# Modulation in four turns of two feature tiles, with w_cond as the moving operand of float32 products

## The chip, the cores and the metric

The kernel runs on one core of one Trainium2 chip. The core has TensorE (PE in the profile, with its weight loads as PEld), VectorE (DVE), ScalarE (ACT), GpSimd (POOL) and SyncE (SP, which here only issues DMAs), each with a queue of its own that it works off in order, and 16 DMA engines. The metric is the device time of one execution in microseconds, as the median of several runs.

## The reference, cut to what matters

One layer of a decoder step: 1024 prompt rows and 8 sample rows go through a modulation, a wide input projection, and two branches (stick-breaking attention and a state-space layer), which are merged and normalised. The change touches the modulation alone:

```python
def _modulate(x, c, w_cond, b_cond):
    mod = c @ w_cond + b_cond
    shift, scale, gate = jnp.split(mod, 3, axis=-1)
    h = x * (1.0 + scale[:, None]) + shift[:, None]
    return h, gate[:, None]

def _project_in(h, w_in):
    z = h @ w_in
    q, k, v, g_att, u, g_ssm, m_att, m_ssm = jnp.split(z, IN_SPLITS, axis=-1)
```

All is float32; `c` has 9 rows here (one for the prompt, eight for the samples), `w_cond` is 1024 x 3072, of which shift and scale take the first 2048 columns, and `w_in` is 1024 x 8192.

## The kernel before

Activations lie transposed: eight feature tiles `xt` of 128 features x 1032 tokens. After the modulation each is split into two reduced-precision parts, `hi` (a cast on ACT) and `lo` (source minus `hi`, on DVE), by `split_act` (L233), and the projection works with three products: hi x hi, hi x lo, lo x hi. A **job** (`gemm`, L125) makes 128 output features: 72 products with 344 moving columns, nine for each feature tile, into three PSUM tiles `pj`. `Weights` (L93) loads a job's weight slab `w32` (one buffer), casts it to `whi` on ACT and subtracts `wlo` on DVE (two buffers each). `Stream` (L148) hands products of the jobs out: `begin(n)` opens the first n jobs, `head(n)` issues products of them out of turn, `drain` and `weave` do the rest, between the steps of the later stages. The first four jobs are q, k, v and gate of the first head pair.

The modulation (`modulate`, L242) runs in two halves. A half takes eight slabs of `w_cond`, each 256 rows by 512 columns, splits each into `wchi` (ACT) and `wclo` (DVE), and multiplies them with a fixed 128-column stationary `csplit`, which holds `c` in its hi part (columns 0 to 8) and its lo part (columns 32 to 40): 32 products of 512 moving columns for a half. The result, rows `mod`, is copied out by ACT (`modr`, L270), turned into features by small products with the selection `sel` that also add hi and lo rows (`pm`, L277), and applied: `md` (L281, L282) is bias plus value, `xt` is scaled and shifted (L285 on ACT for odd tiles, L287 on DVE for even ones, the sample columns at L288 and L289), and `split_act` makes the two parts. In the second half five products of the first job stand behind each slab (`FILL`), and ten more ahead of `features`; they use the first four feature tiles, `job[1] < KT * 9 // 2`.

PE's order is the order in which the program is written. The other engines' orders are made by the scheduler from readiness and priority, and `high_priority(HURRY)` puts a row ahead. Beside the modulation `ssm_tables` (`tabs`, L350 on) makes tables for the state-space layer out of small DVE steps, POOL products over 1056 columns, and two sines on ACT (L428, L429); its three parts are advanced by `next(tabs)`.

Behind the modulation the first job's result is copied out by ACT (`z`, L581), cast to `qs` (L586), its rest subtracted on POOL (L587); the second job gives `kh` (L611) and, on POOL, `kl` (L613), whose upper or lower half a DMA moves to the other partitions (L614). The first score product of the attention, `z` at L661, needs `kl`.

Of the kernel before, what the change touches and what calls it, by code (L numbers as in the profile page):

```python
# [26 lines left out]
LN_EPS = 1e-5  # L27
MAGIC = 12582912.0
MM = 146.0
W32 = 1  # L30
LAG = 2
EDGE = 2
ORDER = {3: (3, 0, 1, 2), 0: (0,), 2: (0, 2, 1), 1: (1, 0)}
HURRY = 400
WCB = 8
ONACT = (1, 3, 5, 7)
FILL = 5
WQ = "pps"
QUEUES = "sasssasss"
PACE = 155  # L40
# [2 lines left out]
GS = "v"  # L43
LATE = 5.0
AHEAD = 2
FILL2 = 10
DRAIN = 1.6
EARLY = 2
TWO_PI = 6.283185307179586
MULT = [float(j) for j in range(9)] + [8.0 * j for j in range(16)] + [128.0 * j for j in range(8)]  # L50
NM = len(MULT)
# [33 lines left out]
def blk(i, w=128):  # L85
    return slice(w * i, w * i + w)
# [6 lines left out]
class Weights:  # L93


    def __init__(self, nc, pool, bufs, ahead):
        self.nc, self.pool, self.bufs, self.ahead = nc, pool, bufs, ahead
        self.todo, self.ready, self.eng, self.q = deque(), deque(), nc.vector, nc.sync

    def plan(self, slabs):  # L100
        self.todo.extend(slabs)

    def emit(self):
        nc = self.nc
        w32 = self.pool.tile([128, KT * 128], F32, tag="w32", bufs=W32, name="w32")
        self.q.dma_start(w32, self.todo.popleft())
        whi = self.pool.tile([128, KT * 128], F32R, tag="whi", bufs=self.bufs, name="whi")
        wlo = self.pool.tile([128, KT * 128], F32R, tag="wlo", bufs=self.bufs, name="wlo")
        nc.scalar.copy(whi, w32)  # L109
        self.eng.tensor_tensor(wlo, w32, whi.bitcast(F32), ALU.subtract)  # L110
        self.ready.append((whi, wlo))
# [36 lines left out]
class Stream:  # L148
# [24 lines left out]
    def head(self, n):  # L173

        for job in self.begun:
            while n and job[1] < KT * 9 // 2:
                next(job[0])
                job[1] += 1
                n -= 1
                self.left -= MM  # L180
                self.clock += MM

# [59 lines left out]
def modulate(k, sp, ps, io, tabs):  # L242


    nc, S = k.nc, k.stream
    PE, ACT, DVE, SP = nc.tensor, nc.scalar, nc.vector, nc.sync
    ct = sp.tile([128, KT, 9], F32, name="ct", bufs=1)
    SP.dma_start(ct, io["ct"])
    cc = split_c(k, sp, ct)
    todo = deque((q, 1024 * s + 512 * half) for half in range(2) for s in range(2) for q in range(4))  # L250
    ahead, xs = deque(), {}

    def load():
        if todo:
            q, c0 = todo.popleft()
            ahead.append(cond_load(k, sp, io, q, c0, WCB))

    def load_x(half):
        for t in range(4 * half, 4 * half + 4):
            xs[t] = sp.tile([128, NT], F32, tag="xt", bufs=5, name="xt")  # L260
            SP.dma_start(xs[t], io["xt"][t])

    def rows(fill):
        ps_ = ps.tile([128, 512], F32, tag="mod", name="mod")
        for q in range(4):
            cond_product(k, ps_, cc, q, cond_split(k, sp, ahead.popleft(), 2))
            load()
            fill()
        r = sp.tile([64, 512], F32, tag="modr", bufs=2, name="modr")
        ACT.copy(r, ps_[0:64])  # L270
        return r

    def features(half, rs):
        pm = ps.tile([128, 512], F32, tag="mod", name="pm")[:, 0:128].rearrange("p (i s n) -> p i s n", i=4, s=2)
        for i in range(4):
            for s in range(2):
                PE.matmul(pm[:, i, s, 0:9], rs[s][:, blk(i)], sel, start=True, stop=True)  # L277
        for i in range(4):
            t = 4 * half + i
            md = sp.tile([128, 2, 9], F32, tag="md", bufs=2, name="md")  # L280
            DVE.tensor_scalar(md[:, 0], pm[:, i, 0, 0:9], bc[:, t:t + 1], None, op0=ALU.add)  # L281
            DVE.tensor_scalar(md[:, 1], pm[:, i, 1, 0:9], bc[:, 8 + t:9 + t], 1.0, op0=ALU.add, op1=ALU.add)  # L282
            x = xs.pop(t)
            if t in ONACT:
                ACT.activation(x[:, 0:NP], x[:, 0:NP], AF.Identity, scale=md[:, 1, 0:1], bias=md[:, 0, 0:1])  # L285
            else:
                DVE.tensor_scalar(x[:, 0:NP], x[:, 0:NP], md[:, 1, 0:1], md[:, 0, 0:1], op0=ALU.mult, op1=ALU.add)  # L287
            DVE.tensor_tensor(x[:, NP:NT], x[:, NP:NT], md[:, 1, 1:9], ALU.mult)  # L288
            DVE.tensor_tensor(x[:, NP:NT], x[:, NP:NT], md[:, 0, 1:9], ALU.add)  # L289
            k.act_h.append(split_act(k, k.hp, x))  # L290

    for n in range(WCB):
        if n == EARLY:
            next(tabs)
        load()
    sel = sp.tile([64, 9], F32, name="sel", bufs=1)
    SP.dma_start(sel, io["sel"])
    bc = sp.tile([128, 16], F32, name="bc", bufs=1)
    SP.dma_start(bc, io["bc"])
    next(tabs)  # L300
    load_x(0)
    k.w.ahead = 2
    k.w.ensure()
    SP.dma_start(k.ident, io["ident"])
    SP.dma_start(k.hb, io["sb_bias"].broadcast_to((128, H)))
    r = [rows(lambda: None) for _ in range(2)]
    features(0, r)
    load_x(1)
    k.w.ahead = 0
    S.begin(2)  # L310
    r = [rows(lambda: S.head(FILL)) for _ in range(2)]
    S.head(FILL2)
    features(1, r)
    S.head(72)
    k.w.ahead = 1


def split_c(k, sp, ct, tag="csplit"):

    nc = k.nc  # L320
    cc = sp.tile([128, KT, 128], F32R, name="csplit", tag=tag, bufs=1)
# [12 lines left out]
def cond_split(k, sp, w, bufs):
    hi = sp.tile([128, 2, 512], F32R, tag="wchi", bufs=bufs, name="wchi")
    lo = sp.tile([128, 2, 512], F32R, tag="wclo", bufs=bufs, name="wclo")
    k.nc.scalar.copy(hi, w)
    k.nc.vector.tensor_tensor(lo, w, hi.bitcast(F32), ALU.subtract)
    return hi, lo


def cond_product(k, ps_, cc, q, parts):

    for t in range(2):
        for x in parts:
            k.nc.tensor.matmul(ps_, cc[:, 2 * q + t], x[:, t], start=(q == 0 and t == 0 and x is parts[0]),
                               stop=(q == 3 and t == 1 and x is parts[1]))
# [1372 lines left out]
```

## Time and profile before

| what | value |
|---|---|
| median of 3 runs | 1664.44 us (1662.58 to 1669.14) |
| the profiled execution's own time | 1668.55 us |
| span of its trace, first to last instruction | 1666.5 us |
| mean granted TensorE clock | 0.958 |
| ACT busy | 754.0 us (45%) |
| DVE busy | 1265.3 us (76%) |
| POOL busy | 895.0 us (54%) |

A row of a timeline gives the start and the duration in us, the engine, the source line, the operation, output and inputs, the count, and in brackets how long the engine had been idle and on whom it waited. A row of a group gives the count behind an x, the busy time in us with the mean in ns, and the idle time ahead of it. In a table by stages, each engine has its busy us and number of instructions, and the last three columns are the granted clock, the busy share of the DMA engines, and GB/s.

### The profile page before, as it was taken

What the parts mean: (1) busy time and instruction counts of PE and PEld (TensorE: products, weight loads), DVE (VectorE), ACT (ScalarE), POOL (GpSimd) and SP (SyncE); (2) the same over time, 40 slices, a digit from 0 to 9 for tenths busy, and PEclk for the clock granted to TensorE, in tenths of its full rate; (3) what the DMA queues carried; (4) which work ended last, traced back from release to release, by engine and by line L of the source; (5) the groups of instructions that cost most, each with busy time, mean ns of one, the idle gap of its engine ahead of it and who ended that gap; (6) DMA issues with size and microseconds to landing.
All of it is one profiled execution on the core that took longest, in us unless ns stands there. A gap on an engine that the chain in (4) does not pass through costs nothing.

```text
span 1666.5 us, 26016 instructions
## 1 busy us (share of the span) xinstructions
PE 1497.7 (90%) x9257; PEld 1423.4 (85%) x9257; DVE 1265.3 (76%) x2342; ACT 754.0 (45%) x1380; POOL 895.0 (54%) x744
## 2 busy tenths in 40 slices
PE   4899899999999999999989898987988869999997
PEld 3799898989898989899978888887878869999885
DVE  8748888888888888872688878978559994544566
ACT  4466666666676666663333333333352222321200
POOL 3437676767676767664456555456336542122154
PEclk8899999999999999999999999889989989999998
DMA  9233333333333333326689888768355576754322
GB/s 333 71 100 82 81 81 81 81 81 81 82 81 82 81 81 81 81 88 205 214 274 292 261 256 266 256 200 233 113 181 172 188 266 240 250 182 150 105 89 89
DMA packets 164125, 258.72 MB, mean 155 GB/s; under 512 B 45049, under 2 KB 106233, under 8 KB 163867
## 3 DMA queue, kind: packets, MB, share of 16 engines
q1 hardware_dynamic: 137945, 163.62, 32.5%
q0 software_dynamic: 23456, 84.95, 15.9%
q10 hardware_dynamic: 2594, 8.49, 1.9%
q8 instruction: 73, 1.20, 0.3%
q14 instruction: 57, 0.47, 0.1%
HBM read 188.38 MB, written 57.86 MB: 148 GB/s over the span
## 4 chain that ended last, share of the span: by engine, by line
PE 41%; DVE 25%; issue 8%; DMA 5%; ACT 4%; POOL 2%; SPq 0%; DVEq 0%; ACTq 0%; POOLq 0%
PE pj L142 26%; PE f L1403 6%; DVE l_t L895 4%; DVE s_sc L837 3%; DVE ke L672 3%; PE o L707 3%; PE tp L690 2%; DMA s_t<-in_cache_k,s_idx 2%; PE z L661 2%; DVE vs L643 2%; DVE be L673 2%; DVE s_t L832 1%; DMA w<-in_w_in 1%; DVE m L1255 1%; DVE ox L716 1%
## 5 line engine op out<-in xcount | busy, mean ns | idle before, releaser
L142 PE MATMUL pj<-ahi,whi 128*128 128x344 f32 x2112 | 700.9, 333 | 56.9 <-ACT u L981 20.4
L142 PE MATMUL pj<-alo,whi 128*128 128x344 f32 x2112 | 691.3, 329 | 10.3 <-DVE alo L1231 5.8
L142 PE MATMUL pj<-ahi,wlo 128*128 128x344 f32 x2112 | 585.0, 329 | 14.2 <-POOL wlo L110 14.2
L142 PEld LDWEIGHTS pj<-ahi,whi 128*128 128x128 f32 x2112 | 410.3, 194 | 65.6 <-ACT u L981 21.4
L142 PEld LDWEIGHTS pj<-alo,whi 128*128 128x128 f32 x2112 | 410.5, 194 | 15.3 <-DVE alo L1231 6.9
L142 PEld LDWEIGHTS pj<-ahi,wlo 128*128 128x128 f32 x2112 | 385.0, 193 | 17.6 <-POOL wlo L110 15.8
L672 DVE TENSOR_TENSOR_SCAN ke<-ke,eye 128x896 f32<-128x896 f32 (+7 forms) x128 | 214.2, 1674 | 81.9 <-ACT ke L662 81.5
L110 POOL TENSOR_TENSOR wlo<-w,whi 128x1024 fp32r<-128x1024 f32 x53 | 134.2, 2532 | 242.7 <-ACT whi L109 242.4
L109 ACT CAST whi<-w 128x1024 fp32r<-128x1024 f32 x90 | 94.9, 1055 | 162.0 <-PE pj L142 111.3
L662 ACT ACTIVATE ke<-z,nhb 128x448 f32<-128x448 f32 (+2 forms) x192 | 112.0, 583 | 82.6 <-PE z L661 79.2
L673 DVE TENSOR_TENSOR be<-be,ke 128x896 f32<-128x896 f32 (+7 forms) x128 | 128.3, 1003 | 11.7 <-DVE ke L672 0.5
L837 DVE SCALAR_TENSOR_TENSOR s_sc<-s_t,s_q,s_sc 128x512 f32<-128x512 f32 x126 | 112.4, 892 | 22.0 <-issue 9.9
L663 ACT ACTIVATE be<-z,hb 128x448 f32<-128x448 f32 (+2 forms) x192 | 110.7, 577 | 0.0
L816 POOL DMA_INDIRECT s_t<-in_cache_k,s_idx x64 | 71.3, 1114 | 39.8 <-issue 12.8
L690 PE MATMUL tp<-ident,be 128*128 128x128 f32 x576 | 89.4, 273 | 0.0
L495 POOL TENSOR_TENSOR pr<-tab 128x256 f32<-128x256 f32 x32 | 31.1, 972 | 102.4 <-DMA tab<-d_tab 98.8
L693 ACT CAST wthi<-tp 128x512 fp32r<-128x512 f32 x96 | 56.6, 590 | 54.7 <-PE tp L690 52.6
L895 DVE SCALAR_TENSOR_TENSOR l_t<-l_t,l_sc 128x128 f32<-128x128 f32 x256 | 78.5, 366 | 2.3 <-DMA l_t<-in_cache_v,l_idx 2.3
L496 POOL TENSOR_TENSOR pt<-tab 128x256 f32<-128x256 f32 x64 | 77.8, 1216 | 3.1
L574 POOL TENSOR_TENSOR sg<-sg,zg 128x1024 f32<-128x1024 f32 x8 | 22.0, 2746 | 99.2 <-ACT sgs L573 99.2
L1525 ACT ACTIVATE gate<-pj 128x344 f32<-128x344 f32 x72 | 33.0, 459 | 92.2 <-PE pj L142 90.1
L661 PE MATMUL z<-kl,qs 128*128 128x448 f32 (+2 forms) x192 | 66.7, 348 | 3.0 <-DMA kl<-kl 3.0
(320 smaller groups left out, 2865.6 us busy)
## 6 DMA issues: line engine op xcount, KB each, us to landing
w<-in_w_in SPq DMA_DIRECT2D x38, 512.0 KB
w<-in_w_in POOLq DMA_DIRECT2D x26, 512.0 KB
wc<-in_w_cond SPq DMA_DIRECT2D x24, 512.0 KB
gst<-d_gg SPq DMA_DIRECT2D x8, 576.0 KB
x<-in_xr SPq DMA_DIRECT2D x9, 512.0 KB
xt<-in_xt SPq DMA_DIRECT2D x8, 516.0 KB
d_ma<-gate SPq DMA_DIRECT2D x8, 516.0 KB
d_mm<-gate SPq DMA_DIRECT2D x8, 516.0 KB
```

The costliest lines, as they stand in the source:

```text
L109: nc.scalar.copy(whi, w32)
L110: self.eng.tensor_tensor(wlo, w32, whi.bitcast(F32), ALU.subtract)
L142: PE.matmul(ps[c], w[:, blk(t)], x[:, cs(c)], start=(t == 0 and i == 0), stop=(t == KT - 1 and i == 2))
L661: nc.tensor.matmul(z[:, 0:wide], st["q", h][:, blk(i)], x[:, s:s + wide], start=j == 0, stop=j == 1)
L662: nc.scalar.activation(ke[:, s:s + cw], z[:, 0:cw], AF.Sigmoid, bias=k.nhb[:, hd:hd + 1], scale=-0.125)
L663: nc.scalar.activation(be[:, s:s + cw], z[:, 0:cw], AF.Sigmoid, bias=k.hb[:, hd:hd + 1], scale=0.125)
L672: nc.vector.tensor_tensor_scan(rev, rev, self.eye[:, NP - n:][:, ::-1], 0.0, ALU.mult, ALU.add)
L673: nc.vector.tensor_tensor(be, be, ke[:, 1:n + 1], ALU.mult)
L690: PE.transpose(tp[:, 2 * order[a] + e], w[e][:, blk(2 * j + a)], k.ident)
L837: DVE.scalar_tensor_tensor(sc, t, q[:, d - d0:d - d0 + 1], sc, op0=ALU.mult, op1=ALU.add)
L895: nc.vector.scalar_tensor_tensor(t[:, d], t[:, d], 1.0, self.sc, op0=ALU.mult, op1=ALU.mult, accum_out=self.acc[:, j, 8 * c + d:8 * c + d ...
L1403: PE.matmul(pp[c], a[:, token(i)], w[:, blk(c, 512)], start=(t == 0 and a is ah and w is wh), stop=(t == KT - 1 and a is al))
```

## The change

The modulation goes in four turns of two feature tiles. For each turn `load` brings four slabs of `w_cond`, 512 rows by 256 columns, and the two `xt` tiles; twelve slabs and six tiles fit at once. The slabs are not split: they are the moving operand of float32 products whose stationary is the nine columns of `ct`, 16 products of 256 columns for a turn (`product`). The rows are copied out with priority, turned by four small products, and one DVE row with priority makes all values of the turn (`turn`); the scale and shift of the prompt columns is on ACT for all eight tiles. In turns 1 to 3, 18 products of the first two jobs stand between `product` and the small products and 18 behind them, nine a job. The second weight slab is loaded into a tile of the setup pool, so that both slabs are loaded and split early. The three parts of `tabs` start later in the written order.

```diff
     def emit(self):
         nc = self.nc
-        w32 = self.pool.tile([128, KT * 128], F32, tag="w32", bufs=W32, name="w32")
+        self.stage.append(self.stage.pop(0))
+        w32 = self.stage[0].tile([128, KT * 128], F32, tag="w32", bufs=1, name="w32")
...
         for job in self.begun:
-            while n and job[1] < KT * 9 // 2:
+            while job[1] < n:
                 next(job[0])
                 job[1] += 1
-                n -= 1
...
-    cc = split_c(k, sp, ct)
...
+    def load(g):
+        for s in range(2):
+            for half in range(2):
+                w = ws[s, half, g] = sp.tile([128, 4, 256], F32, tag="wc", bufs=WCB, name="wc")
+                c0 = 1024 * s + 256 * g
+                SP.dma_start(w, io["w_cond"][512 * half:512 * half + 512, c0:c0 + 256].rearrange("(t p) f -> p t f",
+                                                                                                 p=128))
+        for t in (2 * g, 2 * g + 1):
+            xs[t] = sp.tile([128, NT], F32, tag="xt", bufs=XTB, name="xt")
             SP.dma_start(xs[t], io["xt"][t])
...
+    def product(g):
         ps_ = ps.tile([128, 512], F32, tag="mod", name="mod")
-        for q in range(4):
-            cond_product(k, ps_, cc, q, cond_split(k, sp, ahead.popleft(), 2))
-            load()
-            fill()
...
+        for s in range(2):
+            for t in range(KT):
+                PE.matmul(ps_[0:9, blk(s, 256)], ct[:, t], ws[s, t // 4, g][:, t % 4], start=t == 0, stop=t == KT - 1)
+        rows[g] = sp.tile([9, 512], F32, tag="modr", bufs=2, name="modr")
+        with k.tc.high_priority(HURRY):
+            ACT.copy(rows[g], ps_[0:9])
+
+    def turn(g):
+        pm = ps.tile([128, 512], F32, tag="mod", name="pm")[:, 0:36].rearrange("p (i s n) -> p i s n", i=2, s=2)
+        for s in range(2):
+            for i in range(2):
+                PE.matmul(pm[:, i, s], rows[g][:, blk(2 * s + i)], sel, start=True, stop=True)
+        md = sp.tile([128, 2, 2, 9], F32, tag="md", bufs=2, name="md")
+        with k.tc.high_priority(HURRY):
+            DVE.tensor_tensor(md, pm, bcs[:, 2 * g:2 * g + 2].unsqueeze(3).broadcast_to([128, 2, 2, 9]), ALU.add)
+        for i in range(2):
+            x = xs.pop(2 * g + i)
+            ACT.activation(x[:, 0:NP], x[:, 0:NP], AF.Identity, scale=md[:, i, 1, 0:1], bias=md[:, i, 0, 0:1])
+            DVE.tensor_tensor(x[:, NP:NT], x[:, NP:NT], md[:, i, 1, 1:9], ALU.mult)
+            DVE.tensor_tensor(x[:, NP:NT], x[:, NP:NT], md[:, i, 0, 1:9], ALU.add)
             k.act_h.append(split_act(k, k.hp, x))
...
+    load(0)
...
+    k.w.ahead = 2
+    k.w.stage.append(sp)
+    k.w.ensure()
+    k.w.stage.remove(sp)
+    load(1)
     next(tabs)
+    load(2)
...
+    product(0)
+    turn(0)
+    load(3)
     k.w.ahead = 0
     S.begin(2)
-    r = [rows(lambda: S.head(FILL)) for _ in range(2)]
-    S.head(FILL2)
-    features(1, r)
-    S.head(72)
+    for g in range(1, 4):
+        product(g)
+        S.head(18 * g - 9)
+        turn(g)
+        S.head(18 * g)
+        if g == 1:
+            next(tabs)
     k.w.ahead = 1
```

Three places show the new orders. The first is PE's beginning. Before, this is where the first half ends and the second begins: the last split product of the first half, the eight small products, the first slab of the second half, and the first products of a job (`pj`).

```order
L346 MATMUL mod<-wclo,csplit 128x512
L277 MATMUL pm<-sel,modr 128x9 x8
L346 MATMUL mod<-wchi,csplit 128x512
L346 MATMUL mod<-wclo,csplit 128x512
L346 MATMUL mod<-wchi,csplit 128x512
L346 MATMUL mod<-wclo,csplit 128x512
L142 MATMUL pj<-ahi,whi 128x344
L142 MATMUL pj<-alo,whi 128x344
L142 MATMUL pj<-ahi,wlo 128x344
```

In the changed kernel these are PE's first rows (L263 is `product`, L272 the small products, L140 a job's product):

```order
L263 MATMUL mod<-wc,ct 9x256 x16
L272 MATMUL pm<-sel,modr 128x9 x4
L263 MATMUL mod<-wc,ct 9x256 x16
L140 MATMUL pj<-ahi,whi 128x344
L140 MATMUL pj<-alo,whi 128x344
L140 MATMUL pj<-ahi,wlo 128x344
```

Ahead of the first product of a job there stood 32 split products for the first half and four for the second, and now 32 float32 products.

The second place is ACT at the end of the first two jobs; `pj_408` to `pj_410` are the first job's results before, `pj_506` and `pj_507` the second's, and `qs` is what POOL waits for.

```order
L581 COPY z32_686<-pj_408 128x344
L581 COPY z32_686<-pj_409 128x344
L581 COPY z32_686<-pj_410 128x344
L586 CAST qs_690<-z32_686 64x1024
L586 CAST qs_693<-z32_686 64x1024
L602 COPY zs_696<-z32_686 128x8
L581 COPY z32_740<-pj_506 128x344
L581 COPY z32_740<-pj_507 128x344
```

In the changed kernel `pj_247` to `pj_249` are the first job's, `pj_259` to `pj_261` the second's:

```order
L578 COPY z32_625<-pj_247 128x344
L578 COPY z32_625<-pj_248 128x344
L578 COPY z32_625<-pj_249 128x344
L578 COPY z32_661<-pj_259 128x344
L578 COPY z32_661<-pj_260 128x344
L578 COPY z32_661<-pj_261 128x344
L583 CAST qs_629<-z32_625 64x1024
L583 CAST qs_632<-z32_625 64x1024
```

The casts to `qs` have moved from ahead of the second job's copies to behind them.

The third place is DVE ahead of the last values of the modulation. Before, `md_534` is the first of the second half, and the rows ahead of it (`sm`, L453 to L461) are small steps of the tables.

```order
L338 TENSOR_TENSOR wclo_498<-wc_338,wchi_497 128x1024
L453 TENSOR_SCALAR sm23_602<-tab_117 128x32
L454 TENSOR_TENSOR sm24_603<-sm23_602,sm1_118 128x32
L456 TENSOR_TENSOR sm24_603<-sm24_603,sm25_604 128x32
L457 TENSOR_TENSOR sm26_605<-sm24_603,sm22_601 128x32
L459 TENSOR_TENSOR sm25_604<-sm23_602,sm2_119 128x32
L458 TENSOR_TENSOR sm24_603<-tab_117,sm1_118 128x32
L460 TENSOR_TENSOR sm24_603<-sm24_603,sm25_604 128x32
L461 TENSOR_TENSOR sm27_606<-sm24_603,sm22_601 128x32
L281 TENSOR_SCALAR md_534<-pm_525,bc_141 128x9
```

In the changed kernel `md_519` holds the values of the last turn; `tg_371` and `tt_372` are 1056-column steps of the tables, and `tab_152` (L434) is a product that POOL makes behind the first sine.

```order
L234 TENSOR_TENSOR alo_456<-xt_172,ahi_455 128x1032
L422 TENSOR_SCALAR tg_371<-tf_370 128x1056
L376 TENSOR_SCALAR tt_372<-tg_371 128x1056
L434 TENSOR_SCALAR tab_152<-tab_152 128x32x9
L452 TENSOR_TENSOR sm25_561<-tab_152,sm2_154 128x32
L275 TENSOR_TENSOR md_519<-pm_514,bcs_123 128x36
L279 TENSOR_TENSOR xt_224<-xt_224,md_519 128x8
L279 TENSOR_TENSOR xt_226<-xt_226,md_519 128x8
```

The slabs' splits are gone from DVE, and two rows of the tables that wait for POOL now stand directly ahead of the last values.

More of the change, by code (lines that the diff above doesn't have):

```diff
@@ L29 @@
 MM = 146.0
-W32 = 1
 LAG = 2
@@ L34 @@
 HURRY = 400
-WCB = 8
-ONACT = (1, 3, 5, 7)
-FILL = 5
+WCB = 12
+XTB = 6
 WQ = "pps"
@@ L45 @@
 AHEAD = 2
-FILL2 = 10
 DRAIN = 1.6
-EARLY = 2
 TWO_PI = 6.283185307179586
@@ L98, in __init__ @@
         self.todo, self.ready, self.eng, self.q = deque(), deque(), nc.vector, nc.sync
+        self.stage = [pool]
     def plan(self, slabs):
@@ L248, in modulate @@
     SP.dma_start(ct, io["ct"])
-    cc = split_c(k, sp, ct)
[L250 to L260, printed above, removed]
+    ws, xs, rows = {}, {}, {}
@@ L261, in load_x @@
             SP.dma_start(xs[t], io["xt"][t])
-    def rows(fill):
+    def product(g):
         ps_ = ps.tile([128, 512], F32, tag="mod", name="mod")
-        for q in range(4):
-            cond_product(k, ps_, cc, q, cond_split(k, sp, ahead.popleft(), 2))
-            load()
-            fill()
[L269 to L289, printed above, removed]
-            k.act_h.append(split_act(k, k.hp, x))
@@ L292, in modulate @@
[L292 to L297, printed above, removed]
+        for s in range(2):
[4 more added lines that the diff above has]
+            ACT.copy(rows[g], ps_[0:9])
@@ L298, in modulate @@
+    load(0)
     bc = sp.tile([128, 16], F32, name="bc", bufs=1)
     SP.dma_start(bc, io["bc"])
+    bcs = sp.tile([128, KT, 2], F32, name="bcs", bufs=1)
+    DVE.tensor_copy(bcs[:, :, 0], bc[:, 0:KT])
+    DVE.tensor_scalar(bcs[:, :, 1], bc[:, KT:], 1.0, None, op0=ALU.add)
+    sel = sp.tile([9, 9], F32, name="sel", bufs=1)
+    SP.dma_start(sel, io["sel"][0:9])
+    k.w.ahead = 2
[3 more added lines that the diff above has]
+    load(1)
     next(tabs)
-    load_x(0)
@@ L302, in modulate @@
-    k.w.ahead = 2
-    k.w.ensure()
+    load(2)
     SP.dma_start(k.ident, io["ident"])
     SP.dma_start(k.hb, io["sb_bias"].broadcast_to((128, H)))
-    r = [rows(lambda: None) for _ in range(2)]
-    features(0, r)
-    load_x(1)
+    product(0)
+    turn(0)
+    load(3)
     k.w.ahead = 0
     S.begin(2)
-    r = [rows(lambda: S.head(FILL)) for _ in range(2)]
-    S.head(FILL2)
-    features(1, r)
-    S.head(72)
+    for g in range(1, 4):
[5 more added lines that the diff above has]
+            next(tabs)
```

## The prediction

> **What bounds the kernel now.** I read the page's busy line and the shares of its chain of waits first.
>
> ```profile
> PE 1497.7 (90%) x9257; PEld 1423.4 (85%) x9257; DVE 1265.3 (76%) x2342; ACT 754.0 (45%) x1380; POOL 895.0 (54%) x744
> PE 41%; DVE 25%; issue 8%; DMA 5%; ACT 4%; POOL 2%; SPq 0%; DVEq 0%; ACTq 0%; POOLq 0%
> ```
>
> PE is busy nine tenths of the span, so most of the kernel can't be moved by a change of the modulation. Next I cut the front into windows at the ends of its stages (first split products, second slabs, first `features`, second half, end of the first job, first score product; two of the seven rows are left out).
>
> ```profile
> 0.00:16.00 16.00, 8.41 (x17) 5.22 (x17) 9.56 (x27) 7.01 (x7) 0.20 (x4) 1.00 0.81 268
> ...
> 24.40:38.70 14.30, 0.79 (x1) 0.29 (x1) 14.23 (x34) 9.07 (x9) 9.43 (x4) 0.57 1.04 382
> 38.70:62.40 23.70, 17.91 (x68) 15.21 (x69) 19.52 (x16) 10.96 (x11) 14.12 (x8) 0.76 0.23 78
> 62.40:80.50 18.10, 16.49 (x96) 15.69 (x96) 13.65 (x35) 8.07 (x9) 8.72 (x9) 0.91 0.26 101
> ...
> 97.10:140.00 42.90, 42.86 (x272) 42.35 (x273) 28.35 (x30) 30.73 (x62) 17.37 (x18) 0.96 0.18 55
> ```
>
> PE (the second number) is idle in the front: 7.6 us of the first 16, 13.5 of 24.4 to 38.7, where DVE is busy 14.23 of 14.30. From 97.1 on it is full: 42.86 of 42.90. So the hinge is the end of the front, and I ask the timeline what ends it.
>
> ```profile
> 82.81 4.86 POOL L587 TENSOR_TENSOR qs<-z,qs 64x1024 fp32r<-64x1024 f32 x2 [10.53 <-issue]
> 87.89 5.58 POOL L613 TENSOR_TENSOR kl<-z,kh 64x1024 fp32r<-64x1024 f32 x2 [0.21 <-ACT kh L611]
> 97.14 0.44 PE L661 MATMUL z<-kl,qs 128*128 128x448 f32 x1 [3.04 <-DMA kl<-kl]
> ```
>
> POOL idles 10.53 us, takes `qs` at 82.81, then `kl`; a DMA moves `kl`, and PE waits 3.04 us for it until 97.14. From POOL's `qs` to that product it is 14.3 us, and this stretch stays as it is. All orders behind it are the old ones. So I date the new POOL `qs` and shift the end by the difference, one for one.
>
> **The change part by part.** Removed on DVE and ACT are the splits and casts of 16 slabs.
>
> ```profile
> L338 DVE TENSOR_TENSOR wclo<-wc,wchi 128x1024 fp32r<-128x1024 f32 x16 | 21.6, 1358 | 5.1 <-ACT wchi L337 5.0
> L346 PE MATMUL mod<-wclo,csplit 128*128 128x512 f32 x32 | 17.6, 550 | 12.8 <-DVE wclo L338 12.6
> L346 PE MATMUL mod<-wchi,csplit 128*128 128x512 f32 x32 | 16.8, 526 | 15.4 <-ACT wchi L337 15.4
> L337 ACT CAST wchi<-wc 128x1024 fp32r<-128x1024 f32 x16 | 16.7, 1044 | 17.5 <-PE mod L346 11.3 <-DMA wc<-in_w_cond 6.3
> ```
>
> DVE loses 21.6 us, ACT 16.7, and PE 64 split products (34.4 us of busy time). Their waits, 12.8 and 15.4 us behind DVE and ACT, go with them. PE gains 64 float32 products of 256 columns. None stands in this trace; the nearest rows have 512 columns, and two records each, so that one float32 product appears as two.
>
> ```profile
> 8.56 0.63 PE L346 MATMUL mod<-wclo,csplit 128*128 128x512 f32 x1
> 8.99 0.63 PE L346 MATMUL mod<-wchi,csplit 128*128 128x512 f32 x1
> 20.22 0.40 PE L346 MATMUL mod<-wclo,csplit 128*128 128x512 f32 x1
> 20.46 0.39 PE L346 MATMUL mod<-wchi,csplit 128*128 128x512 f32 x1
> 1197.45 1.02 PE L1160 MATMUL ycr<-gst,ssr 128*128 128x512 f32 x2
> 1198.31 1.02 PE L1160 MATMUL ycr<-tt,ni 128*128 128x512 f32 x2
> 1200.21 1.02 PE L1168 MATMUL ypk<-ec,pick 128*8 128x512 f32 x2 [0.88 <-DVE ec L1163]
> ```
>
> From start to start a split product takes 0.43 us early and 0.24 later: the clock is at half speed in the beginning. A float32 product of 512 columns takes 0.86 (1197.45 to 1198.31), also 1.02 with a stationary of eight columns, so 256 columns should take half of 0.86: **0.43 at full clock, 0.86 at half**. A turn of 16 is 6.9 or 13.8 us; all 64 are 27.5 or 55.
>
> Next the slabs, since products now wait for DMA alone.
>
> ```profile
> 5.18 1.04 ACT L337 CAST wchi<-wc 128x1024 fp32r<-128x1024 f32 x1 [3.08 <-DMA wc<-in_w_cond]
> DMA packets 828, 1.60 MB, mean 399 GB/s; under 512 B 48, under 2 KB 48, under 8 KB 828
> DMA packets 753, 1.05 MB, mean 263 GB/s; under 512 B 48, under 2 KB 560, under 8 KB 753
> ```
>
> The first slab is there at 5.18. The DMA rows are the windows 10:14 and 91:95. A slab of 0.52 MB in 2 KB runs takes 0.52 MB / 399 GB/s = 1.3 us. The new slabs have runs of 1 KB; the nearest window, with 560 of 753 packets below 2 KB, moved 263 GB/s, so 2.0 us is the upper bound. I take 1.5, nearer to the first, because the second window was not asked for more than it moved. The last slab of turn 1 lands behind seven new slabs, two weight slabs and two `xt` tiles, the latter four also 0.5 MB each: 5.2 + 7 x 1.5 + 4 x 1.33 = 21.0 (19.6 to 24.5 with the bounds).
>
> Now the walk. Rows for its steps:
>
> ```profile
> L270 ACT COPY modr<-mod 64x512 f32<-64x512 f32 x4 | 2.3, 580 | 4.0 <-PE mod L346 4.0
> 64.66 1.95 PE L277 MATMUL pm<-sel,modr 64*128 64x9 f32 x16
> L285 ACT ACTIVATE xt<-xt,md 128x1024 f32<-128x1024 f32 x4 | 5.0, 1240 | 9.8 <-DVE md L282 9.8
> L236 ACT CAST ahi<-xt 128x1032 fp32r<-128x1032 f32 x8 | 8.1, 1051 | 1.8 <-DVE xt L289 1.8
> L581 ACT COPY z<-pj 128x344 f32<-128x344 f32 x6 | 2.5, 447 | 0.1
> L237 DVE TENSOR_TENSOR alo<-xt,ahi 128x1032 fp32r<-128x1032 f32 x8 | 9.5, 1221 | 0.0
> 79.47 0.32 PE L142 MATMUL pj<-ahi,whi 128*128 128x344 f32 x1
> 79.63 0.32 PE L142 MATMUL pj<-alo,whi 128*128 128x344 f32 x1
> 98.63 0.49 PE L142 MATMUL pj<-alo,whi 128*128 128x344 f32 x1
> 98.92 0.49 PE L142 MATMUL pj<-ahi,wlo 128*128 128x344 f32 x1
> ```
>
> 1. Turn 0: 8 products at half clock and 8 at full are 10.3 us, from 5.2 to **15.5** (14.0 to 19 if the clock rises sooner, or not at all). The copy 0.58 and the small products 1.0 (half of 1.95, as they are half as many) bring 17.1.
> 2. Turn 1: 17.1 + 6.9 = 24.0 if no slab is late, 27.6 if the last four come at 24.5 and at half clock; I take **25.5**. ACT has scaled and cast turn 0's two tiles by 17.4 + 2 x 1.24 + 2 x 1.05 = 22, and DVE's `alo` follows, so PE's job products find them ready.
> 3. Turns 2 and 3 each take 36 job products at 0.157 (0.16 in the rows), 1.0 for the small ones, and 6.9: 13.6 us. Twice that gives **52.6**. The last 18 job products ahead of the small ones, and these, end at 56.4.
> 4. The last values, `md_519`, now stand on DVE behind two table rows that wait for POOL, which adds some 2 us (estimate from the stalls below): 58.5. The tables themselves wait on the sine at ACT.
>
> ```profile
> 31.66 3.35 POOL L420 TENSOR_TENSOR tf<-tf,tt 128x1056 f32<-128x1056 f32 x1 [4.65 <-DVE tt L379]
> 32.64 2.40 DVE L289 TENSOR_TENSOR xt<-xt,md 128x8 f32<-128x8 f32 x1
> 60.85 0.87 POOL L435 TENSOR_TENSOR tab<-t_mg,tg 128x288 f32<-128x288 f32 x1 [5.86 <-ACT tg L429]
> ```
>
> An eight-column row of DVE took 2.40 us beside a POOL row of 3.35, until this ended (35.0): one such stall is up to 2.4 us, and nothing at best. The scheduler's rows still put POOL beside the turns.
> 5. The last two tiles: two scalings and two casts on ACT (2 x 1.24 + 2 x 1.05 = 4.6), `alo` 1.22 and one part of a stall, 0.7: **65**.
> 6. Of the two jobs 33 products are left that need those tiles: 5.2 us at 0.157, 9.5 at 0.287 (98.63 to 98.92). PE has waited since about 59 and its clock will have fallen, as in the row of 24.4 to 38.7, where it stood at 0.57 with PE idle. Half at each is 7.5: **72.7**.
> 7. The casts to `qs` have moved behind the second job's three copies, so they wait for both jobs, not for one. That is the loss in the change, the second job's 18 products of step 6 (2.8 to 5 us), counted there. A copy (0.45) and a cast (1.05) later POOL begins `qs` at about **74**.
>
> The second weight slab's own tile costs 1.3 us of DMA early, counted above; its split goes on ACT and DVE where the slabs' are gone. Moving the scaling of all tiles to ACT adds four of 1.24 there, and is in steps 2 and 5; its cover is the 16.7 us that ACT lost.
>
> Sum: 82.8 - 74 = 8.8, rounded to 9 us gained. Without stalls, and with the clock full in steps 2 and 6, it would be 13 to 14 (2 from step 4, 2.3 from step 6). The profiled execution took 1668.55, its span 1666.5 and 2.05 around it, and lies 4.1 above the median of 1664.44; I subtract from the median: **1655.4**.
>
> **The rivals.**
>
> *The clock stays down (slower).* A float32 product with only nine columns of stationary may not keep the clock up. Rows of the stretch in which the small float32 products ran:
>
> ```profile
> 63.74:67.16 3.42, 3.42 (x27) 3.19 (x26) 2.20 (x6) 0.00 (x0) 3.22 (x4) 1.00 0.00 0
> 67.16:70.57 3.41, 3.41 (x14) 3.41 (x13) 3.41 (x6) 2.13 (x2) 3.25 (x3) 0.52 0.00 0
> ```
>
> PE is shown 100% busy in the first, 1.95 us of it with small nine-column products, and the clock is 0.52 in the next. If nine columns count as idle, 56 products that I have at full clock cost 0.43 more each, 24 us; turns 1 to 3 have job products between, which raise the clock again, and waits that hide some, so about 18 come through: a loss of 9, 1673. It becomes slower than before once more than 21 products (9 / 0.43) run at half clock beyond my eight. Against it: the row 1200.21 with eight columns lasted 1.02, as with 128. I give it 0.11. The Trainium skill, "TensorE: Matmul & The Clock Gate", Part 1, says that a busy window of about 3.4 us raises the clock and an idle one lowers it, whatever runs; by it this rival is out and the forecast stands. Part 4 of the same page says that transposes don't count as busy in the same way; were it so for these products, too, the sum would be the 1673 of this rival. The row of 63.74 speaks against the first as the profile counts busy, so I keep the chance.
>
> *The tables hold the tail.* `tabs` starts later, POOL's rows behind the sine took from 60.85 until POOL's 10.53 us of idle before `qs`, so to 72.3, before, and ACT must do the sine between the scalings. If the sine comes 4 us later than the last turn needs, `md_519`, or POOL's `qs` behind the tables, is late by as much: gain 4, **1660**. For it stand the two rows ahead of `md_519`; against it, DVE has lost 21.6 us and makes the tables sooner. 0.20.
>
> *It changes nothing.* Were something else than the chain to `kl` the limit at 97, such as POOL's order, the end stays: 1664. PE's 3.04 us wait for `kl` speaks against. 0.07.
>
> *All goes well.* No stall and full clock, as worked out: 1651. 0.12.
>
> **How the numbers follow.** The forecast has 0.50, with 6.5 to 12.5 us for its own range (1652 to 1658): the DMA bounds move step 2 by 2 either way, and stalls and clock the tail by 2 each. A measurement of this kernel can tell about 0.5%, 8.3 us, from no change. Of the forecast's 0.50 some 0.6 lies above that, 0.30; with 0.12 of the good case and a little of the tables' that is 0.43 for faster. Slower by over 8.3 is most of the clock rival, 0.09. The rest, 0.48, is the same. The range leaves out the clock rival and half of the far end of the good case: 1649 to 1667.
>
> **What would show it.** The profile after should have no idle on PE that ends at DVE or ACT before 25 us; float32 records that are 0.43 apart per product from about 12 us on; the last small products at 56, `md` behind them by 2; POOL's `qs` at 74 and the first score product near 88, with PE full behind it. Twice 0.43 beyond 16 us is the clock rival; a sine behind 50 us on ACT and POOL without idle ahead of `qs` is the tables'. It is wrong if the time after the first score product isn't the old one less what came before: then something behind it sets the end.

## The result and the profile after

The changed kernel took 1650.32 us (median of 4 runs, 1647.58 to 1653.41) against 1664.89 for the kernel before (4 runs): a ratio of 0.991, 95% interval 0.9883 to 0.9937. Measured once more with five rounds it was 1652.43 against 1663.13, a ratio of **0.9939, interval 0.9922 to 0.9956**, which is 7 to 13 us. The profiled execution took 1650.37, its span 1648.7. The forecast was 1655.4 in a range of 1649 to 1667.

The page of the changed kernel, in the lines that were shown of before:

```profile
PE 1507.8 (91%) x9321; PEld 1422.5 (86%) x9321; DVE 1236.3 (75%) x2309; ACT 741.8 (45%) x1368; POOL 893.4 (54%) x744
PE 26%; DVE 18%; DMA 7%; issue 4%; POOL 3%; ACT 2%; SPq 1%; DVEq 0%; ACTq 0%; POOLq 0%
```

DVE lost 29 us and ACT 12, PE gained 10. The shares of the chain of waits have changed far more than the time has; they say where the chain was followed, and are no measure of a gain. The table by stages (the columns are those of before; the stages are first turn, second turn, third, fourth, last small products, first two jobs, score product):

```profile
0.00:13.80 13.80, 8.77 (x32) 3.22 (x32) 0.42 (x5) 1.34 (x2) 0.20 (x4) 1.00 0.85 308
13.80:23.40 9.60, 8.00 (x41) 3.79 (x40) 5.33 (x10) 6.78 (x7) 0.00 (x0) 1.00 1.07 380
23.40:37.50 14.10, 14.10 (x78) 9.45 (x77) 12.24 (x55) 4.84 (x5) 4.95 (x2) 1.00 0.97 335
37.50:51.60 14.10, 14.10 (x78) 9.47 (x77) 12.32 (x20) 6.71 (x7) 8.98 (x5) 1.00 0.42 165
51.60:58.60 7.00, 7.00 (x45) 6.52 (x44) 3.51 (x13) 3.77 (x5) 5.69 (x5) 1.00 0.00 0
58.60:73.60 15.00, 10.72 (x48) 10.15 (x48) 6.90 (x13) 7.01 (x12) 9.55 (x8) 0.77 0.34 131
73.60:87.50 13.90, 7.26 (x49) 6.90 (x48) 1.23 (x1) 6.86 (x9) 11.76 (x6) 0.86 0.62 169
```

From 16.4 to 58.6 PE is full, at full clock. The idle time is now at the two ends. The timeline's rows that carry the forecast's steps, in order of time:

```profile
5.03 8.80 PE L263 MATMUL mod<-wc,ct 128*9 128x256 f32 x32 [5.03 <-DMA wc<-in_w_cond]
15.44 1.05 PE L272 MATMUL pm<-sel,modr 9*128 9x9 f32 x8 [1.60 <-ACT modr L266]
16.42 7.07 PE L263 MATMUL mod<-wc,ct 128*9 128x256 f32 x32
54.56 1.05 PE L272 MATMUL pm<-sel,modr 9*128 9x9 f32 x8
55.18 0.94 DVE L434 TENSOR_SCALAR tab<-tab 128x288 f32<-128x288 f32 x1 [3.35 <-POOL tab L433]
56.77 0.18 DVE L275 TENSOR_TENSOR md<-pm,bcs 128x36 f32<-128x36 f32 x1
60.81 3.23 DVE L234 TENSOR_TENSOR alo<-xt,ahi 128x1032 fp32r<-128x1032 f32 x2
68.22 1.04 ACT L107 CAST whi<-w 128x1024 fp32r<-128x1024 f32 x1 [6.97 <-PE pj L140]
73.63 5.91 POOL L584 TENSOR_TENSOR qs<-z,qs 64x1024 fp32r<-64x1024 f32 x2 [4.96 <-ACT qs L583]
87.52 0.71 PE L658 MATMUL z<-kl,qs 128*128 128x448 f32 x1 [6.66 <-DMA kl<-kl]
```

POOL takes `qs` at 73.63 (forecast 74) and the first score product with `kl` runs at 87.52 (forecast 88): **9.62 us earlier than the 97.14 of before**. But the two profiled spans differ by 17.8 us. The other 8 us lie far behind the front, in the state-space stage, where PE waits for ACT's copies of `u`, `gate` and `zgate`. The table of PE's waits there (us in total, times, longest), before and after:

```profile
PE pj L142 <- ACT u L981: 20.4, 5, 7.5
PE pj L142 <- ACT zgate L1527: 18.1, 4, 10.5
PE pj L142 <- ACT gate L1525: 5.9, 1, 5.9
```

```profile
PE pj L140 <- ACT u L978: 16.8, 5, 6.7
PE pj L140 <- ACT zgate L1524: 13.4, 4, 8.0
PE pj L140 <- ACT gate L1522: 3.3, 1, 3.3
```

They fell from 44.4 to 33.5 us though every engine's order there is the same. So there were two questions: is that part of the gain, and which part of the change makes the 9.6 us?

### The profile page after: what moved, and what is told of

Read it like the earlier page. It is cut to its first block, busy times and chain, and to the rows that moved or that the text cites. A ratio compares the mean times of both kernels' runs of the same rounds, so it can differ in the third digit from the quotient of the medians.

```text
span 1648.7 us, 26067 instructions
## 1 busy us (share of the span) xinstructions
PE 1507.8 (91%) x9321; PEld 1422.5 (86%) x9321; DVE 1236.3 (75%) x2309; ACT 741.8 (45%) x1368; POOL 893.4 (54%) x744
## 4 chain that ended last, share of the span: by engine, by line
PE 26%; DVE 18%; DMA 7%; issue 4%; POOL 3%; ACT 2%; SPq 1%; DVEq 0%; ACTq 0%; POOLq 0%
PE pj L140 18%; PE f L1400 6%; DVE l_t L892 4%; DVE s_sc L834 3%; DMA w<-in_w_in 2%; DMA s_t<-in_cache_k,s_idx 2%; DVE s_t L829 1%; DVE m L1252 1%; DVE xs L1045 1%; POOL s_t L813 1%; PE o L704 1%; POOL wlo L108 1%; DMA s_t<-in_cache_v,s_idx 1%; DVE alo L234 1%; DVE sr L1036 1%
## 5 line engine op out<-in xcount | busy, mean ns | idle before, releaser
L140 PE MATMUL pj<-ahi,whi 128*128 128x344 f32 x2112 | 701.0, 333 | 49.2 <-ACT u L978 16.8
L140 PE MATMUL pj<-alo,whi 128*128 128x344 f32 x2112 | 691.8, 329 | 10.2 <-DVE alo L234 5.4
L140 PE MATMUL pj<-ahi,wlo 128*128 128x344 f32 x2112 | 584.6, 329 | 14.1 <-POOL wlo L108 14.1
L140 PEld LDWEIGHTS pj<-ahi,whi 128*128 128x128 f32 x2112 | 410.1, 194 | 59.6 <-ACT u L978 17.8
L140 PEld LDWEIGHTS pj<-alo,whi 128*128 128x128 f32 x2112 | 410.4, 194 | 14.8 <-DVE alo L234 6.6
L140 PEld LDWEIGHTS pj<-ahi,wlo 128*128 128x128 f32 x2112 | 385.2, 193 | 17.2 <-POOL wlo L108 15.8
L670 DVE TENSOR_TENSOR be<-be,ke 128x896 f32<-128x896 f32 (+7 forms) x128 | 134.7, 1052 | 10.9
L834 DVE SCALAR_TENSOR_TENSOR s_sc<-s_t,s_q,s_sc 128x512 f32<-128x512 f32 x126 | 109.7, 871 | 20.8 <-DMA s_t<-in_cache_k,s_idx 14.1
L813 POOL DMA_INDIRECT s_t<-in_cache_k,s_idx x64 | 69.9, 1092 | 36.6 <-issue 11.9
L493 POOL TENSOR_TENSOR pt<-tab 128x256 f32<-128x256 f32 x64 | 81.2, 1269 | 3.1
```

The source lines that it names most:

```text
L140: PE.matmul(ps[c], w[:, blk(t)], x[:, cs(c)], start=(t == 0 and i == 0), stop=(t == KT - 1 and i == 2))
L670: nc.vector.tensor_tensor(be, be, ke[:, 1:n + 1], ALU.mult)
L813: nc.gpsimd.indirect_dma_start(out=tile[:, j].rearrange("p d s -> p (d s)"), out_offset=None, in_=self.io["cache_" + what], in_offset=bass ...
L834: DVE.scalar_tensor_tensor(sc, t, q[:, d - d0:d - d0 + 1], sc, op0=ALU.mult, op1=ALU.add)
```

## The experiments

Two numbers of each profile are compared: the start of the first score product with `kl`, and the rest of the span behind it. The ratio is against the kernel before, run on the same chip.

| kernel | ratio, 95% interval | first score product | rest of the span |
|---|---|---|---|
| before | 1 | 97.14 | 1569.4 |
| after | 0.991 (0.9883 to 0.9937) | 87.52 | 1561.2 |
| again_before | 0.9998 (0.9983 to 1.0013) | 97.01 | 1565.4 |
| again_after | 0.9939 (0.9922 to 0.9956) | 87.28 | 1568.2 |
| double | 1.009 (1.0065 to 1.0115) | 107.96 | 1563.3 |
| half | 0.9934 (0.991 to 0.9959) | 88.86 | 1563.4 |
| split | 1.0051 (1.0031 to 1.0071) | 102.26 | 1563.0 |
| onetile | 1.0033 (1.0016 to 1.0051) | 98.95 | 1570.1 |
| twotile | 1.0036 (1.0016 to 1.0055) | 100.44 | 1566.8 |
| tail | 0.9937 (0.9914 to 0.996) | 89.14 | 1567.5 |
| tabs_first | 0.9931 (0.9906 to 0.9957) | 88.54 | 1560.4 |
| tabs_pool | 0.9918 (0.9899 to 0.9938) | 86.13 | 1560.6 |
| tabs_pool_tail | 0.9948 (0.9928 to 0.9968) | 84.19 | 1565.2 |

**Both kernels once more**, without an edit.

> The changed kernel once more, unaltered. Two theories of the time behind the front. Shift: the end moves only by as much as the first score product moves (97.14 to 87.52, 9.6 us), and the rest of the 17.8 us between the two profiled spans is chance in the DMA waits of the state-space stage. Then the ratio to before is 0.994, and in this profile the first score product is again at 87.5 while PE's waits behind the copies of u, gate and zgate in the state-space stage may be anywhere between 33.5 and 44.4 us. More: something of the change also acts behind the front in every run, some 5 to 8 us. Then the ratio is 0.989 to 0.991 and those waits are again near 33.5 us.

> The kernel before once more, unaltered. Shift: the ratio is 1.000, the first score product at 97.1, and PE's waits behind the copies of u, gate and zgate, 44.4 us in the first profile, come out some us elsewhere, down to the 33.5 us of the changed kernel's profile. More: they are near 44 us again.

Shift is right. The score product came at 87.28 and 97.01, within 0.25 us of the first profiles, and the ratio was 0.9939 where 9.7 of 1663 us make 0.9942. The same waits were 38.2 us in the changed kernel this time and 40.6 in the kernel before. The rest of the span was 7 us longer in one profile of the changed kernel than in the other; over all 13 profiles it lies between 1560.4 and 1570.1 and follows neither the change nor the front. The extra 8 us were chance.

**Twice the products, and half of them.**

```diff
-        for s in range(2):
+        for s in (0, 1, 0, 1):
             for t in range(KT):
```

> Every float32 product of the modulation is issued twice, 64 more, and the results are the same. Orders behind the front are those of the changed kernel. If a float32 product of 256 columns costs 0.43 us at full clock and PE sets the pace of the turns, the first score product moves from 87.5 to 115 (64 x 0.43 = 27.5 later), less the 1 us that the first small products wait for ACT now. If the turns waited for slabs or for DVE, it moves by less than 20. Shift: the end moves by the same, to about 1677. More: the end moves by 5 to 8 us more or less than the first score product does.

```profile
22.38 13.98 PE L263 MATMUL mod<-wc,ct 128*9 128x256 f32 x64
81.23 1.05 PE L272 MATMUL pm<-sel,modr 9*128 9x9 f32 x8
85.92 0.42 PE L140 MATMUL pj<-ahi,whi 128*128 128x344 f32 x1 [0.61 <-ACT ahi L233]
93.51 4.86 POOL L584 TENSOR_TENSOR qs<-z,qs 64x1024 fp32r<-64x1024 f32 x2 [27.18 <-ACT qs L583]
107.96 0.71 PE L658 MATMUL z<-kl,qs 128*128 128x448 f32 x1 [4.80 <-DMA kl<-kl]
```

These rows of the doubled kernel's timeline show two things. A turn of 32 products (64 records) takes 13.98 us in place of 7.07, so a float32 product of 256 columns is 0.43, as forecast, and PE sets the pace: the last small products moved by 26.7. But the score product moved by only 20.5, because the tail behind the small products (82.3 to 93.5) is 11.2 us where the changed kernel's (55.6 to 73.6) is 18.0. The expected 27.5 missed that the tables would be over by then (POOL is idle from 66.3 on).

```diff
-            for t in range(KT):
+            for t in range(0, KT, 2):
```

> Half of the modulation's products are left out (the odd feature tiles of the sum); all slabs are still loaded. PE alone would be 13.8 us earlier at the last small products. The slabs and tiles of the last turn are 26 transfers of 0.5 MB, at 1.33 to 1.5 us each in at 38 to 43, so the last product can't end before about 43, 8.5 earlier than now; and POOL is busy with the tables until 68.7, 5 us before it takes qs now. If the tables hold the tail then, the first score product comes 5 us earlier, at 82.5; if neither binds, 13 earlier. Shift: the end moves by the same.

```profile
17.54 6.37 PE L263 MATMUL mod<-wc,ct 128*9 128x256 f32 x16 [2.47 <-DMA wc<-in_w_cond]
71.11 1.04 ACT L107 CAST whi<-w 128x1024 fp32r<-128x1024 f32 x1 [5.26 <-DMA w<-in_w_in]
72.06 2.18 ACT L578 COPY z<-pj 128x344 f32<-128x344 f32 x6
```

With half the products the last small ones ended only 6.5 us earlier (49.1), not 13.8: in the first two turns PE now waits 3.6 us for slabs, and the second runs in part at half clock (6.37 us, where the third and fourth take 3.62). The score product came 1.3 us later. ACT's rows of that kernel show why: the scheduler put the cast of a later weight slab ahead of all six copies, and that slab had not landed. So in the changed kernel the number of products sets the turns, but the slabs are close behind them in the first two, and ACT's order and the tables (POOL is busy with them until 70.9 here) in the tail; with these as they are, cheaper products gain nothing.

**One part of the change at a time.** `split` keeps the turns and goes back to two reduced-precision parts (its edit also lets eight slabs in at once in place of twelve, to make room for the parts); `onetile` takes the second weight slab's tile away; `twotile` gives that tile to the kernel before.

```diff
+                ACT.copy(hi, w)
+                DVE.tensor_tensor(lo, w, hi.bitcast(F32), ALU.subtract)
...
+                        PE.matmul(ps_[:, blk(s, 256)], cc[:, 4 * half + t], x[:, t], start=half == 0 and t == 0 and x is hi,
```

> The four turns stay, but the slabs are split again and multiplied as two reduced-precision parts with the fixed 128-column stationary. If the float32 products are what gains (no cast and no subtraction on the way), the first score product goes back towards 97, with PE waiting for DVE's subtractions in the turns. If it is the turns with the products of two jobs woven in, the split is hidden: a turn then needs 4 x 1.36 + 2 x 1.22 = 8 us of DVE and 4 x 1.04 + 0.6 + 2 x 1.2 + 2 x 1.05 = 9 us of ACT, less than PE's 14.0, and PE itself needs 32 products of half of 0.24 us (3.8) in place of 6.9, so that the first score product stays at 86 to 90.

```diff
-    k.w.stage.append(sp)
     k.w.ensure()
-    k.w.stage.remove(sp)
```

> The changed kernel with one tile for the weight slabs again, so that the second slab waits until the first is split (16 to 17 us) and then comes behind the slabs of later turns. PE needs it at 24.9, for the second job's first products. If that tile matters, PE waits there 2 to 6 us and the first score product is as much later (89 to 93). If not, it stays at 87.4.

```diff
-        w32 = self.pool.tile([128, KT * 128], F32, tag="w32", bufs=W32, name="w32")
+        self.stage.append(self.stage.pop(0))
+        w32 = self.stage[0].tile([128, KT * 128], F32, tag="w32", bufs=1, name="w32")
```

> The kernel before with the second weight slab's own tile alone. In the changed kernel, taking that tile away cost 11.5 us at the first score product. In the kernel before the second job's products begin only behind the second half, at 65 us and later, long after both slabs could be split with one tile; so the first score product stays at 97 and the time within noise of before. If the tile gains by itself, the first score product is earlier by 3 us or more.

The longest waits of PE in the timelines of `split` (with two rows of ACT), then `onetile`, then `twotile`:

```profile
44.56 0.58 PE L271 MATMUL mod<-wclo,csplit 128*128 128x256 f32 x1 [5.10 <-DVE wclo L268]
55.23 2.38 ACT L287 ACTIVATE xt<-xt,md 128x1024 f32<-128x1024 f32 x2 [5.75 <-DVE md L284]
62.27 1.98 ACT L267 CAST wchi<-wc 128x1024 fp32r<-128x1024 f32 x2
63.35 0.58 PE L271 MATMUL mod<-wchi,csplit 128*128 128x256 f32 x1 [5.43 <-ACT wchi L267]
```

```profile
36.61 1.05 ACT L107 CAST whi<-w 128x1024 fp32r<-128x1024 f32 x1 [10.40 <-DMA w<-in_w_in]
37.71 0.65 PE L140 MATMUL pj<-ahi,whi 128*128 128x344 f32 x1 [10.49 <-ACT whi L107]
```

```profile
35.70 0.80 PE L350 MATMUL mod<-wchi,csplit 128*128 128x512 f32 x1 [10.23 <-ACT wchi L341]
100.44 0.44 PE L665 MATMUL z<-kl,qs 128*128 128x448 f32 x1 [3.09 <-DMA kl<-kl]
```

Splitting the slabs in the turns brings PE's waits for DVE and ACT back, and the score product comes 15 us later than in the changed kernel, 5 later than before. The sum of DVE and ACT time for a turn, 8 and 9 us, had said that it would be hidden. But these rows don't run beside the products at will. The subtraction that the first wait shown is for starts at 43.30, behind two `alo` in DVE's queue, one of which took 3.07 us beside POOL. The cast behind the second wait (62.27) stands in ACT's queue behind a wait of 5.75 us for `md`, the two scalings, the two casts and the first sine; other casts wait for PE to leave one of two buffers, 12.2 us in all. The eight slabs matter little: ACT's casts wait 3.1 us in all for slabs.

Without the second tile PE waits 10.49 us for the second slab, which SP issues only at 26.87, and then runs at half clock (0.50 to 0.58 in 37.7 to 48), so that the last small products end 17.7 us later (73.3). The tail takes 11.2 us there, too, and so the score product is 11.4 us later than in the changed kernel, where I had expected 2 to 6. The tile alone is a loss, too: in the kernel before it puts ACT's cast of the second slab (32.53) ahead of that of the second half's first `w_cond` slab (34.62, where it was 31.89 in `again_before`), and the second half's first product comes at 35.70 in place of 32.98. So by the first score product, against before, the order with float32 products loses 1.8 us without the tile, the tile loses 3.3 without that order, and the order loses 5.1 without float32 products; together they make 9.6. Float32 products in the old order of two halves were not run, and the scaling of all tiles on ACT was not taken apart.

**The tail.** Two ideas to shorten it: products with the lo part last, and the tables earlier.

```diff
-    order += ends(range(KT - EDGE, KT))
+        order += [(t, c, i) for t in range(KT - EDGE, KT) for c in range(NC3) for i in (0, 2)]
+        order += [(t, c, 1) for c in range(NC3) for t in range(KT - EDGE, KT)]
```

> The changed kernel with the last two feature tiles of the first two jobs in another order: all products with the hi parts first, those with the lo part last. In the changed kernel PE waits 1.3 us for alo twice there and then runs 20 products at half clock. If these waits set when POOL gets qs, the first job is complete at 64.5 in place of 68.3 and the second at 67.4 in place of 72.5, and the first score product comes 3 to 5 us earlier, no more since POOL has the tables until 68.7. If ACT's order or POOL sets it, it comes less than 1.5 us earlier. Shift: the end moves by the same.

The score product came 1.6 us later, at 89.14: as in `half`, ACT's next row was the cast of a slab that landed only at 71.3, ahead of the copies.

```diff
+    next(tabs)
     load(0)
...
     load(1)
-    next(tabs)
     load(2)
```

> The changed kernel with the small loads of the tables issued ahead of the slabs, so that the scheduler puts the tables' steps ahead of the last turns on DVE, POOL and ACT; PE's order is the same. In the doubled kernel, whose tables are over before the last turn, POOL took qs 11.2 us after the last small products (82.3 to 93.5); in the changed kernel it takes 18.0 (55.6 to 73.6). If the tables make that difference (the two rows ahead of the last md, slower rows of DVE beside POOL, the sine on ACT), POOL takes qs at 67, the first score product is at 81 and the end about 6.5 us earlier than the changed kernel's. If it is something else (ACT's order, a late transfer), the first score product stays within 2 us of 87.4. Shift: the end moves by the same as the first score product.

```profile
10.17 9.92 PE L263 MATMUL mod<-wc,ct 128*9 128x256 f32 x32 [10.17 <-DMA wc<-in_w_cond]
61.63 1.05 PE L272 MATMUL pm<-sel,modr 9*128 9x9 f32 x8
73.90 4.83 POOL L584 TENSOR_TENSOR qs<-z,qs 64x1024 fp32r<-64x1024 f32 x2 [13.58 <-issue]
```

The tail is now 62.7 to 73.9, 11.2 us, as in the doubled kernel and in `onetile`: it is where the tables stand against the turns that makes it 18.0. Two things change with it and were not taken apart: DVE and POOL are free in the tail, and on ACT the scheduler now puts the casts to `qs` ahead of the second job's last two copies. But five small loads ahead of the slabs made the first slab 5.1 us late, and the score product came at 88.54.

```diff
-    SP.dma_start(lr, io["a_re"])
+    POOL.dma_start(lr, io["a_re"])
```

(and so for `li`, `ld` and `mult`, on top of the edit above)

> The changed kernel with the tables' small loads issued from POOL's queue at the start, beside the slabs on SP's. With these loads ahead on SP's queue the tail from the last small products to POOL's qs shrank from 18.0 to 11.3 us, but the first slab came at 10.17 in place of 5.03. If the queue made that delay, the first slab is now back at 5 to 6, the last small products at 55 to 56, POOL takes qs at 67, the first score product is at 81, and the end 6 us earlier than the changed kernel's. If the small packets hold up the slabs on whatever queue, the first slab comes at 8 to 10 and the first score product stays at 86 to 88.

```profile
5.40 9.41 PE L263 MATMUL mod<-wc,ct 128*9 128x256 f32 x32 [5.40 <-DMA wc<-in_w_cond]
18.86 9.51 PE L263 MATMUL mod<-wc,ct 128*9 128x256 f32 x32 [2.33 <-DMA wc<-in_w_cond]
86.13 0.71 PE L658 MATMUL z<-kl,qs 128*128 128x448 f32 x1 [4.76 <-DMA kl<-kl]
```

The first slab is back at 5.40, and now the second turn waits for its slabs (2.33 us, and 9.51 for the turn in place of 7.07, since the clock fell to 0.50 in 18.8 to 22.2). It ends 4.9 us later than in the changed kernel (28.4 against 23.5), so the loads cost about as much on POOL's queue, only later. The tail is 11.2 us once more (60.5 to 71.7). The score product gains 1.4 us on the changed kernel, against 6 expected.

> The same, and the last two feature tiles of the first two jobs in the order with the lo parts last. With ACT's order no longer putting a late weight slab's cast ahead of the copies, the products that wait for alo should now be worth what was expected of them: the first score product 1 to 3 us ahead of that of the kernel with POOL's loads alone. If ACT's copies and casts set the tail, within 1 us of it.

With both it came at 84.19, 1.9 us earlier still, as expected. By its profile this is the best front of all, 3.3 us ahead of the changed kernel; by time it is 0.9948, `tabs_pool` 0.9918 and the changed kernel 0.9939, with intervals that overlap. No version is shown to beat the changed kernel; what this one loses elsewhere follows.

**The shift itself.** Worked out from the score product, 9 of the 12 ratios lie in their intervals (`split` on the edge), and the other three (the first measurement of the change, `onetile`, `tabs_pool_tail`) are out by at most 0.0006, 1 us. But an interval is 5 to 9 us wide, and one part of the difference is not chance. In `split`, `onetile`, `twotile` and `tabs_pool_tail` the scheduler also moved rows of DVE, ACT and POOL behind the state-space stage, the same rows in all four; in the other nine profiles the order there is that of before. From the last product into `ysp`, at the end of that stage (L1173 in the changed kernel), to the end of the span it is 459.5 to 460.6 us in those nine, and 466.1, 466.0, 462.7 and 464.9 in the four. PE's waits in that stretch of `onetile` have a row of 4.3 us (3.6 to 4.3 in the four) that none of the nine has:

```profile
PE pj L140 <- ACT sig L1249: 4.3, 3, 1.8
```

So these four lose some 3 to 6 us far behind the front, and their times are 2.7 to 4.3 us longer than the shift gives. For the variants with the old order there, one for one holds less closely than the two kernels themselves suggest: `double` is 4.1 us longer than the shift gives, `half`, `tail`, `tabs_first` and `tabs_pool` are 2.5 to 2.9 shorter, which no trace here explains.

## Why the prediction was right, step by step

**The hinge and the shift.** Right: the end moves as the first score product does as long as the orders behind it stay. The two kernels, run once more, show it within 1 us, the five variants with the old order behind the front within about 4; in the other four variants late rows moved, and the end with them. POOL's `qs` was forecast at 74 and came at 73.63; the gain was forecast at 9 and is 9.6 to 9.7 by the traces, 10.7 by the medians of the longer measurement.

**Steps 1 and 2.** The products of turn 0 took 8.80 us where 10.3 were taken: half clock held for fewer than eight products (the three turns at full clock take 7.07 each, and 1.7 more is four products at twice the price). The following wait for ACT (1.60, behind the cast of a weight slab at 13.74) gave back 1 us of that. Turn 1 ended at 23.4, not 25.5: no slab was late. Of these 2 us, 0.7 come from turn 0 and 1.5 are the allowance for late slabs (25.5 taken for 24.0), which was not needed, since slabs in 1 KB runs are not slower here. (The far bound of that step, 24.5 and four products at 0.86, is 27.9, not 27.6.) The DMA view of the changed kernel's window 4:18:

```profile
DMA packets 4065, 5.41 MB, mean 387 GB/s; under 512 B 333, under 2 KB 3553, under 8 KB 4065
```

With most packets below 2 KB it moved 387 GB/s, 1.35 us for a slab, not the 1.5 taken and far from the bound of 2.0.

**Step 3** was 14.1 us a turn against 13.6, as each of the four changes between kinds of products in a turn costs PE some 0.1.

**Steps 4 and 5.** `md` came 1.2 us behind the small products (2 were taken), and the second `alo` at 64.0 (65). The two `alo` took 1.6 us each beside POOL, and 1.2 in turn 0, where POOL is idle, as the row of the stall led to expect.

**Steps 6 and 7.** PE's clock in the tail, by the table of windows of the changed kernel:

```profile
59.50:62.90 3.40, 1.17 (x4) 0.64 (x4) 3.37 (x4) 1.75 (x2) 3.27 (x3) 1.00 0.00 0
62.90:66.30 3.40, 2.21 (x8) 2.21 (x9) 1.14 (x1) 0.00 (x0) 3.24 (x3) 0.54 0.00 0
66.30:69.70 3.40, 3.40 (x13) 3.40 (x13) 0.40 (x1) 1.48 (x3) 2.29 (x4) 0.50 0.45 191
69.70:73.10 3.40, 3.40 (x22) 3.40 (x22) 1.13 (x6) 2.40 (x6) 0.00 (x0) 0.95 0.91 339
```

One window with PE busy for a third of it, and the clock was half for the next two, the second of which was full: 20 products at 0.29 in place of 0.16, 2.6 us, near the 2.3 taken. From the second `alo` to the end of the second job it was 8.0 us (7.5 taken; 65 and 7.5 make 72.5, not the 72.7 of the forecast). The casts to `qs` behind the second job's copies cost what the forecast said. What it had not seen is the cast of the third weight slab (68.22), which stands ahead of the first job's copies. It cost nothing here, since ACT still waited 0.49 us for PE ahead of the second job's last copy; in `half` and `tail` the cast of the slab after it sets the tail.

**How near, and how much of it is luck.** No step was off by more than some 2 us, but the errors partly cancelled on the way: the end of turn 1 was 2.1 us early, the last small products 0.8 (55.6 against 56.4), `md` 1.6 (56.9 against 58.5) and `qs` 0.4.

**The rivals.** That nine columns leave the clock down was wrong: the third and fourth turns have 1.00, and 16 products take 7.07 us. Of the two rules quoted from the Trainium skill ("TensorE: Matmul & The Clock Gate"), the one of Part 1 fits these turns, and the one on transposes does not apply to such products. In the tail PE was not idle in the window ahead of the fall but busy for 1.17 of 3.40 us. And the row of 63.74 stays open: its small products (64x9) have nine moving columns, not nine stationary ones, so they said nothing about the products of the turns. Behind the same 16 records the clock fell again in `again_before` (0.54 in 67.3 to 70.7) and did not in `twotile` (1.00 in 69.9 to 73.3). The tables, with the order that ACT gets from their place, do hold the tail, by 6.8 us (18.0 against 11.2), more than the 4 that the rival was given; but the forecast's tail of 17.6 (56.4 to 74) already had this in it, so it was no gain lost but one not yet taken.

**What was not seen** is what the second slab's tile is worth. The forecast counted it as 1.3 us of DMA. Without it the change is a loss: the first score product of `onetile` comes 1.8 us later than before, and its ratio is 1.0033, with the late rows in it. The sum came out right because the tile was there; as a statement about the parts it was wrong.

## What to carry to other kernels

Date the first event behind which the bounding engine is full, and forecast that; the rest of the span then moves with it, if the scheduler has left the orders behind it alone, which should be looked at (four of nine variants here lose 3 to 6 us by rows that moved some 1100 us further on). The rest's own spread (10 us here) should be known before a difference there is explained. Ask of every part of a change what happens to the others without it: here the new product, the order of the turns and one tile gain only together. And where a stage is shortened, look for the row that the scheduler has put ahead of the next link in an in-order queue, such as the cast of a weight slab that isn't needed yet.

## What had not been expected of the hardware

The row of granted clock showed 1.00 from the start of the trace while the first products took twice as long (in the changed kernel a record every 0.43 us up to 8.4 us, every 0.22 from 8.7 on); the half clock at the beginning is seen only in the products' own pitch. And the five small loads, some 65 KB, delayed the first slab by 5.1 us. SP's issues of the first slabs in `tabs_first` and in the changed kernel show where 2.8 us of this went:

```profile
4.08 2.08 SPq L253 DMA_DIRECT2D wc<-in_w_cond  x4
1.26 2.07 SPq L253 DMA_DIRECT2D wc<-in_w_cond  x4
```

SP took 0.4 to 0.6 us to issue each of the small loads. The other 2.3 us lie between the issue and the landing. The DMA view of `tabs_first` and of the changed kernel, window 2:10:

```profile
DMA packets 1793, 1.22 MB, mean 153 GB/s; under 512 B 677, under 2 KB 1793, under 8 KB 1793
```

```profile
DMA packets 2336, 2.68 MB, mean 335 GB/s; under 512 B 151, under 2 KB 2199, under 8 KB 2336
```

Less than half of the bytes moved in the window where 677 packets were below 512 B; how much of that is the late issue and how much the small packets was not taken apart.
